# A two-layer attention, Hyena and RWKV-7 step on one core: TensorE's instructions pinned to the source's order

## The chip, the cores and the metric

The kernel runs on one core of a Trainium2 chip. The core has five engines that each work through an instruction stream of their own: TensorE (matmuls and transposes), VectorE and ScalarE (elementwise work), GpSimd (here mainly memsets and DMA issues) and SyncE (here DMA issues). They meet through semaphores. In the profile they are PE, DVE, ACT, POOL and SP. The metric is the device time of one execution in microseconds.

## The reference

One inference step of a backbone with two layers, on 128 context tokens and 128 latent tokens of width 2048, in fp32. The part that matters:

```python
def _layer(x, cond, p, ctx):
    sh1, sc1, g1, sh2, sc2, g2 = _modulation(cond, p['ada_w'], p['ada_b'])   # silu(cond) @ ada_w + ada_b, 6 vectors
    h = _rmsnorm(x, nw[0]) * (1.0 + sc1) + sh1
    o, st = _mixer(h, p, ctx)
    x = x + g1 * _rmsnorm(o, nw[1])
    h = _rmsnorm(x, nw[2]) * (1.0 + sc2) + sh2
    f = jnp.square(jax.nn.relu(h @ p['mlp_w1'])) @ p['mlp_w2']
    return x + g2 * _rmsnorm(f, nw[3]), st

def _mixer(h, p, ctx):
    u = h @ p['w_in']                       # one input projection
    att = ...   # 12 heads, 4 kv heads, softmax with a sink
    hy = _hyena(u_hy, p)                    # long convolution; its filter is sin(sin(feat @ f1) @ f2) @ f3
    rw, S_fin = _rwkv(...)                  # 12 heads, a scan over 128 tokens in each direction
    return jnp.concatenate([att, hy, rw], -1) @ p['w_out'], ...
```

## The kernel before

Both token groups are handled together, as two sets of 128 rows. A weight product is done in three passes, since each fp32 operand is split into a rounded high part and a rest: `acth` and `actl` (or `osh`, `osl`, `fh`, `fl`) for activations, `wh` and `wl` for weights. `wload` brings a block of weights by DMA from SyncE into `wr`; ScalarE rounds it to `wh` (line 219) and VectorE subtracts to get `wl` (line 220). `ws` (lines 481 to 501) multiplies with 256 columns per matmul, `as_` (lines 503 to 519) with 512. Both are generators that yield after each contraction tile. Their results are the PSUM tiles `mm`, of which there are two; all small steps use `sm` tiles, of which there are three.

The stages follow each other: boot (modulation vectors of layer 0 and the first norm), mixer 0, norm, MLP 0, norm, mixer 1, norm, MLP 1. A norm (line 455) works in eight groups: VectorE scales a piece `xn`, TensorE transposes it in four instructions (line 466), and ScalarE and VectorE make `acth` and `actl` from it. The products of the next stage need all eight groups only for their last contraction tiles.

In a mixer the weight products are the main stream, and everything small runs beside it. `Side` holds generators for the small chains: the Hyena filter (line 550: a matmul, a sine, a matmul, a sine, two matmuls at lines 567, 571 and 579), attention, the Hyena convolution, and RWKV. `run` (line 1089) walks through a weight product and after each contraction tile calls `Side.step`, which lets the generators write their next piece, and `ada_step`, which writes the modulation matmuls (`ada`, lines 374 to 376, eight at a time with 32 output rows each). The rates stand in `OPTS` (line 108). A generator that yields a number is left alone for so much work of the main stream.

RWKV goes in two batches of three blocks of 128 channels per layer. `rwkv_stage1` (line 804) does a block: low-rank products (lines 820 and 828), a chain of tanh, running sums and exponentials on VectorE and ScalarE, two small matmuls (lines 845 and 850), two scaled copies `rkf` (line 874), their transposes (line 880), and products of 64-row tiles (line 904, four in a group). `rwkv_stage2` (line 980) then reads the inverted blocks back as `rXT` by DMA and runs groups of 32 by 32 tiles (lines 1001 and 1003); `rwkv_out` (line 1033) normalises and transposes the result (line 1061).

This source order is not the order of execution. A scheduler takes the program as written with its data dependences and its own estimate of durations, and may put instructions of an engine in another order where no dependence stands against it. Before, that holds for every engine, TensorE too. Each engine then works through its stream in the order given to it.

Of the kernel before, what the change touches and what calls it, by code (L numbers as in the profile page):

```python
# [18 lines left out]
KT = 16  # L19
# [137 lines left out]

class Kern:
    def __init__(self, tc, es, A, O, opts=None):
# [6 lines left out]
        self.side = Side()  # L166
        self.adaq = deque()
# [56 lines left out]
    def setup(self):  # L224
# [17 lines left out]
        nc.tensor.transpose(ps[:, 0:32], th[:], self.ident[0:32, 0:32])  # L242
# [21 lines left out]
    def params(self, l):  # L264
# [34 lines left out]
        for i, gr in enumerate(groups):  # L299
# [3 lines left out]
            nc.tensor.transpose(ps[:, 0:n], rows[:], self.ident[0:n, 0:n])  # L303
# [17 lines left out]
    def ada_group(self, l, P, i, cg):  # L321
# [4 lines left out]
        for kq in range(8):  # L326
# [5 lines left out]
            else:  # L332
                w.append(t)
                for j in range(4):
                    m = nc.tensor.matmul(ps[32 * j:32 * j + 32, :], lhsT=self.cs[:, 2 * (kq - 1) + j, :], rhs=w[j // 2][:, j % 2, :],
                                         start=(kq == 1), stop=(kq == 7))
# [6 lines left out]
        for j in range(4):  # L343
            nc.tensor.matmul(pv[:, j, :], lhsT=rows[:, j * 128:(j + 1) * 128], rhs=self.cst("selq"), start=True, stop=True)
# [16 lines left out]
    def ada_vector(self, l, P, i):  # L361
# [4 lines left out]
        for k in range(KT):  # L366
            for h in range(2):
# [3 lines left out]
                if len(w) == 4:  # L371
                    for kk in (k - 1, k):
                        for j in range(4):
                            nc.tensor.matmul(ps[32 * j:32 * j + 32, :], lhsT=self.cs[:, kk, :],  # L374
# [17 lines left out]
        else:  # L392
# [4 lines left out]
            for q in range(4):  # L397
                nc.tensor.matmul(pv[:, q], lhsT=rows[:, q * 128:(q + 1) * 128], rhs=self.cst("sel8").rearrange("p (j c) -> p j c", c=2),
# [56 lines left out]
    def norm(self, P, parts, isc, ish, act):  # L455
# [3 lines left out]
        for c in range(4):  # L459
            for g in range(2):  # L460
# [4 lines left out]
                for j in range(4):  # L465
                    nc.tensor.transpose(pv[:, j, :], xn[:, j * 128:(j + 1) * 128], self.ident)
# [14 lines left out]
    def ws(self, act, w, widths, ps):  # L481
# [4 lines left out]
        for kq in range(KT // nk):  # L486
            hi, lo = self.wload(w[kq * nk * 128:(kq + 1) * nk * 128, :], nk, ncol)
            for kk in range(nk):
# [3 lines left out]
                for b, wd in enumerate(widths):  # L492
                    o = ps[0:wd, b * 256:(b + 1) * 256]
                    h, lw = hi[:, kk, c0:c0 + wd], lo[:, kk, c0:c0 + wd]
                    m = nc.tensor.matmul(o, lhsT=h, rhs=hh, start=(k == 0 and b % 2 == 0), stop=False, skip_group_check=True)  # L495
                    if b == 0 and kk == 0:
                        self.anchors.append(m.ins.name)
                    nc.tensor.matmul(o, lhsT=h, rhs=hl, start=False, stop=False, skip_group_check=True)  # L498
                    nc.tensor.matmul(o, lhsT=lw, rhs=hh, start=False, stop=(k == KT - 1), skip_group_check=True)  # L499
# [3 lines left out]
    def as_(self, lhs, ks, w, ncol, ps):  # L503
# [3 lines left out]
        for i0 in range(0, len(ks), nk):  # L507
            hi, lo = self.wload(w[ks[i0] * 128:(ks[i0] + nk) * 128, :], nk, ncol)
            for kk in range(nk):
                first, last = i0 + kk == 0, i0 + kk == len(ks) - 1  # L510
                for g in range(2):
                    hh, hl = (a[:, g * 128:(g + 1) * 128] for a in lhs[ks[i0 + kk]])
                    o = ps[:, g * 512:g * 512 + ncol]
                    m = nc.tensor.matmul(o, lhsT=hh, rhs=hi[:, kk, :], start=first, stop=False)  # L514
                    if g == 0 and kk == 0:
                        self.anchors.append(m.ins.name)
                    nc.tensor.matmul(o, lhsT=hh, rhs=lo[:, kk, :], start=False, stop=False)  # L517
                    nc.tensor.matmul(o, lhsT=hl, rhs=hi[:, kk, :], start=False, stop=last)  # L518
# [31 lines left out]
    def hyena_filter(self, l):  # L550
# [16 lines left out]
        nc.tensor.matmul(ps[0:64, 0:128], lhsT=f1[:], rhs=self.cst("featt")[0:33, :], start=True, stop=True)  # L567
# [3 lines left out]
        nc.tensor.matmul(ps[0:64, 0:128], lhsT=f2[:], rhs=h1[:], start=True, stop=True)  # L571
# [799 lines left out]
```

## Time and profile before

| what | value |
|---|---|
| median of 3 runs | 2949.42 us (2944.27 to 2960.29) |
| the profiled execution, its own time | 2948.62 us |
| its span in the trace | 2946.8 us |
| TensorE busy | 2833.7 us, 96% of the span |
| VectorE busy | 1651.4 us, 56% |
| ScalarE busy | 1230.8 us, 42% |
| GpSimd busy | 177.5 us, 6% |
| mean DMA rate | 222 GB/s |

The profiled execution lies within the spread of the runs; 1.8 us of its time lie outside the span. The page gives busy time per engine, the chain of work that ended last, and groups of instructions; the trace behind it can be asked for single instructions with start and duration, with the idle time before them and who ended it, and for the busy time in any stretch. The granted clock is a share of TensorE's full clock of 2.4 GHz: 1.00 is 2.4 GHz and 0.50 is 1.2 GHz. A matmul's duration overlaps the next one's start, so the price of one in a row is the distance between starts.

### The profile page before, as it was taken

How to read it: one execution, taken by the hardware profiler on the slowest of the kernel's cores; microseconds unless marked ns; L12 is line 12 of the kernel's file. 1: busy time of each engine (PE TensorE's matmuls, PEld its weight loads, DVE VectorE, ACT ScalarE, POOL GpSimd, SP SyncE). 2: the span in 40 equal slices, each digit the busy share in tenths (PEclk: the TensorE clock that was granted, in tenths of full speed). 3: DMA queues.
4: the chain of work that ended last, by engine and by line, in shares of the span. 5: the costliest groups of instructions: out<-in, count | busy, mean ns of one | idle time of the engine just before them, and what ended most of it. 6: DMA issues, size and time to landing. Idle time of an engine off the chain costs nothing.

```text
span 2946.8 us, 47852 instructions
## 1 busy us (share of the span) xinstructions
PE 2833.7 (96%) x19163; PEld 2318.8 (79%) x19163; DVE 1651.4 (56%) x2627; ACT 1230.8 (42%) x1870; POOL 177.5 (6%) x368
## 2 busy tenths in 40 slices
PE   6899999999899999999999999999879999999998
PEld 2586787767797797897876978887669989889896
DVE  1356666776654344444446576776775545545555
ACT  2354345434543343343335454453355444444343
POOL 0011101201000000000000111011000000000000
PEclk9999899999999999999999998998889999999999
DMA  9985575477888888888898744533455666666674
GB/s 337 333 296 185 188 253 157 137 258 275 296 280 288 275 287 274 299 283 281 284 334 274 232 135 114 147 93 95 138 189 170 188 187 186 186 187 186 188 240 150
DMA packets 326057, 654.56 MB, mean 222 GB/s; under 512 B 48581, under 2 KB 86030, under 8 KB 325707
## 3 DMA queue, kind: packets, MB, share of 16 engines
q1 hardware_dynamic: 311328, 610.88, 64.0%
q0 software_dynamic: 12928, 36.98, 3.8%
q10 hardware_dynamic: 1579, 3.64, 0.3%
q8 instruction: 150, 2.46, 0.3%
q14 instruction: 72, 0.59, 0.1%
HBM read 632.21 MB, written 19.20 MB: 221 GB/s over the span
## 4 chain that ended last, share of the span: by engine, by line
PE 86%; DVE 5%; DMA 5%; ACT 2%; issue 1%; SPq 0%; POOL 0%; DVEq 0%; ACTq 0%; POOLq 0%
PE mm L495 12%; PE mm L499 12%; PE mm L498 12%; PE mm L514 11%; PE mm L517 11%; PE mm L518 11%; PE ada L374 5%; PE sm L904 2%; DMA wa<-in_ada_w_dram 2%; PE sm L925 1%; PE sm L1003 1%; DVE wl L220 1%; PE sm L1018 1%; PE sm L1001 1%; DMA wr<-in_ada_w_dram 1%
## 5 line engine op out<-in xcount | busy, mean ns | idle before, releaser
L220 DVE TENSOR_TENSOR wl<-wr,wh 128x1024 fp32r<-128x1024 f32 (+1 forms) x784 | 928.1, 1185 | 931.2 <-ACT wh L219 910.0
L219 ACT CAST wh<-wr 128x1024 fp32r<-128x1024 f32 (+1 forms) x784 | 796.5, 1017 | 1169.3 <-PE mm L498 545.6
L495 PE MATMUL mm<-acth,wh 128*128 128x256 f32 (+1 forms) x3200 | 914.4, 286 | 11.5 <-ACT acth L476 9.2
L499 PE MATMUL mm<-acth,wl 128*128 128x256 f32 (+1 forms) x3200 | 907.1, 283 | 2.4 <-DVE wl L220 2.4
L498 PE MATMUL mm<-actl,wh 128*128 128x256 f32 (+1 forms) x3200 | 907.5, 284 | 0.3 <-DVE actl L477 0.3
L495 PEld LDWEIGHTS mm<-acth,wh 128*128 128x128 f32 (+1 forms) x3200 | 605.2, 189 | 56.3 <-issue 23.8
L499 PEld LDWEIGHTS mm<-acth,wl 128*128 128x128 f32 (+1 forms) x3200 | 605.2, 189 | 8.3 <-DVE wl L220 3.4
L498 PEld LDWEIGHTS mm<-actl,wh 128*128 128x128 f32 (+1 forms) x3200 | 605.4, 189 | 3.9 <-issue 2.5
L517 PE MATMUL mm<-wl,fh 128*128 128x512 f32 x1024 | 408.0, 398 | 0.3 <-DVE wl L220 0.3
L514 PE MATMUL mm<-wh,fh 128*128 128x512 f32 x1024 | 406.6, 397 | 0.0
L518 PE MATMUL mm<-wh,fl 128*128 128x512 f32 x1024 | 402.4, 393 | 0.0
L514 PEld LDWEIGHTS mm<-wh,fh 128*128 128x128 f32 x1024 | 191.8, 187 | 67.6 <-ACT wh L219 10.9
L518 PEld LDWEIGHTS mm<-wh,fl 128*128 128x128 f32 x1024 | 192.3, 188 | 45.7
L517 PEld LDWEIGHTS mm<-wl,fh 128*128 128x128 f32 x1024 | 192.4, 188 | 43.8 <-DVE wl L220 0.8
L374 PE MATMUL ada<-wa,cs 128*32 128x512 f32 x1280 | 180.6, 605 | 9.2 <-DMA wa<-in_ada_w_dram 9.1
L514 PE MATMUL mm<-wh,osh 128*128 128x512 f32 x256 | 108.8, 425 | 3.4 <-ACT osh L1172 3.4
L517 PE MATMUL mm<-wl,osh 128*128 128x512 f32 x256 | 105.0, 410 | 3.4 <-DVE wl L220 3.4
L518 PE MATMUL mm<-wh,osl 128*128 128x512 f32 x256 | 103.0, 402 | 0.0
L374 PEld LDWEIGHTS ada<-wa,cs 128*32 128x32 f32 x1280 | 35.3, 109 | 84.9 <-issue 54.2
L904 PE MATMUL sm<-rZR,rKB 64*128 64x256 f32 x384 | 83.8, 456 | 0.7 <-DVE rLA L908 0.3
L514 PE MATMUL mm<-wh,acth 128*128 128x512 f32 (+1 forms) x192 | 74.8, 389 | 0.0
L517 PE MATMUL mm<-wl,acth 128*128 128x512 f32 (+1 forms) x192 | 69.1, 360 | 0.0
(323 smaller groups left out, 2598.2 us busy)
## 6 DMA issues: line engine op xcount, KB each, us to landing
wr<-in_mlp_w_dram SPq DMA_DIRECT2D x512, 512.0 KB
wa<-in_ada_w_dram SPq DMA_DIRECT2D x352, 512.0 KB
wr<-in_w_in_dram SPq DMA_DIRECT2D x96, 512.0 KB
wr<-in_w_in_dram SPq DMA_DIRECT2D x112, 384.0 KB
wr<-in_w_out_dram SPq DMA_DIRECT2D x64, 512.0 KB
wr<-in_ada_w_dram SPq DMA_DIRECT2D x32, 512.0 KB
gb<-gate POOLq DMA_DIRECT2D x16, 512.0 KB, 8.9
xd<-acc SPq DMA_DIRECT2D x24, 256.0 KB
```

Of the source, the lines that this page charges most:

```text
L219: nc.scalar.copy(hi, raw)
L220: nc.vector.tensor_sub(lo, raw, hi)
L374: nc.tensor.matmul(ps[32 * j:32 * j + 32, :], lhsT=self.cs[:, kk, :], rhs=w[2 * (kk - k + 1) + j // 2][:, 512 * (j % 2):512 * (j % 2) + 51 ...
L495: m = nc.tensor.matmul(o, lhsT=h, rhs=hh, start=(k == 0 and b % 2 == 0), stop=False, skip_group_check=True)
L498: nc.tensor.matmul(o, lhsT=h, rhs=hl, start=False, stop=False, skip_group_check=True)
L499: nc.tensor.matmul(o, lhsT=lw, rhs=hh, start=False, stop=(k == KT - 1), skip_group_check=True)
L514: m = nc.tensor.matmul(o, lhsT=hh, rhs=hi[:, kk, :], start=first, stop=False)
L517: nc.tensor.matmul(o, lhsT=hh, rhs=lo[:, kk, :], start=False, stop=False)
L518: nc.tensor.matmul(o, lhsT=hl, rhs=hi[:, kk, :], start=False, stop=last)
L904: nc.tensor.matmul(ps[h][:, i * 256:(i + 1) * 256], lhsT=KB[hs, d, g, i, :], rhs=ZR[hs, d, g, :, :].rearrange("p i t -> p (i t)"), start=T ...
L925: nc.tensor.matmul(o[:, 64 * h:64 * h + 64], lhsT=R.MA[d][h][:, 0:128] if i == 0 else MY[h][:], rhs=vT[:, g, 64 * h:64 * h + 64], start=fi ...
L1001: nc.tensor.matmul(o, lhsT=LA[d][:, gh, qs[d]], rhs=G[:, d, gh, :], start=True, stop=True)
```

## The change

A small class `Ordered` wraps `nc.tensor.matmul` and `nc.tensor.transpose`. Each instruction issued through it gets an edge to the one issued before it. The edge is of order alone (`NoSync`): it emits no semaphore and no wait, it only tells the scheduler that the second may not be put ahead of the first. Every matmul and transpose of the kernel is now called as `self.te.matmul` or `self.te.transpose`; nothing else is edited. TensorE's stream is so the order in which the source writes it, and the other engines' streams are still the scheduler's.

```diff
+class Ordered:
+    def __init__(self, tc):
+        self.tc, self.last = tc, None
+
+    def queue(self, i):
+        if self.last is not None:
+            self.tc.add_manual_dep(i.ins, self.last, mybir.DependencyInfo(mybir.DependencyClass.NoSync, mybir.DependencyReason.DATA),
+                                   reason="order")
+        self.last = i.ins.name
+        return i
+
+    def matmul(self, *a, **k):
+        return self.queue(self.tc.nc.tensor.matmul(*a, **k))
+
+    def transpose(self, *a, **k):
+        return self.queue(self.tc.nc.tensor.transpose(*a, **k))
...
         self.side = Side()
+        self.te = Ordered(tc)
...
                 for j in range(4):
-                    nc.tensor.transpose(pv[:, j, :], xn[:, j * 128:(j + 1) * 128], self.ident)
+                    self.te.transpose(pv[:, j, :], xn[:, j * 128:(j + 1) * 128], self.ident)
```

The number of matmuls is the same. 13386 of 16811 keep their very position in TensorE's stream; the others move by at most 228 places. The moves lie in the boot, in the two mixers and in the norms. In the changed kernel every matmul is issued from line 172 and every transpose from line 175.

The first place is the norm ahead of the second MLP, on TensorE. `xn` is the scaled piece, `acth`, `actl`, `wh` and `wl` belong to the MLP's first product. Before:

```order
L466 MATMUL sm_20976<-const_66,xn_20974 128x128 x4
L466 MATMUL sm_20990<-const_66,xn_20988 128x128 x4
L466 MATMUL sm_21004<-const_66,xn_21002 128x128 x4
L495 MATMUL mm_21092<-acth_20954,wh_21094 128x256
L466 MATMUL sm_21018<-const_66,xn_21016 128x128 x4
L498 MATMUL mm_21092<-actl_20955,wh_21094 128x256
L499 MATMUL mm_21092<-acth_20954,wl_21095 128x256
L495 MATMUL mm_21092<-acth_20954,wh_21094 128x256
L498 MATMUL mm_21092<-actl_20955,wh_21094 128x256
L499 MATMUL mm_21092<-acth_20954,wl_21095 128x256
L495 MATMUL mm_21092<-acth_20954,wh_21094 128x256
L498 MATMUL mm_21092<-actl_20955,wh_21094 128x256
```

After, at the same place:

```order
L175 MATMUL sm_20976<-const_66,xn_20974 128x128 x4
L175 MATMUL sm_20990<-const_66,xn_20988 128x128 x4
L175 MATMUL sm_21004<-const_66,xn_21002 128x128 x4
L175 MATMUL sm_21018<-const_66,xn_21016 128x128 x4
L175 MATMUL sm_21032<-const_66,xn_21030 128x128 x4
L175 MATMUL sm_21046<-const_66,xn_21044 128x128 x4
L175 MATMUL sm_21060<-const_66,xn_21058 128x128 x4
L175 MATMUL sm_21074<-const_66,xn_21072 128x128 x4
L172 MATMUL mm_21092<-acth_20954,wh_21094 128x256
L172 MATMUL mm_21092<-actl_20955,wh_21094 128x256
```

The products that stood between the last five groups of transposes (55 up to the eighth group) now stand behind all eight.

The second place is the Hyena filter of layer 0, on TensorE. `hf` are its small weights, `hh` is what the sine chain gives. Before, its second matmul stands 60 rows behind the first, among the mixer's first products:

```order
L495 MATMUL mm_1066<-acth_107,wh_1196 128x256
L498 MATMUL mm_1066<-actl_108,wh_1196 128x256
L499 MATMUL mm_1066<-acth_107,wl_1197 128x256
L571 MATMUL sm_1116<-hh_206_1108,hf_199_1081 64x128
L495 MATMUL mm_1066<-acth_109,wh_1233 128x256
L498 MATMUL mm_1066<-actl_110,wh_1233 128x256
```

After:

```order
L172 MATMUL sm_1098<-const_66,hf_198_1079 64x128
L172 MATMUL mm_1066<-acth_103,wh_1068 128x256
L172 MATMUL mm_1066<-actl_104,wh_1068 128x256
L172 MATMUL mm_1066<-acth_103,wl_1069 128x256
L172 MATMUL mm_1066<-acth_103,wh_1068 128x256
L172 MATMUL mm_1066<-actl_104,wh_1068 128x256
L172 MATMUL mm_1066<-acth_103,wl_1069 128x256
L172 MATMUL sm_1116<-hh_206_1108,hf_199_1081 64x128
```

Six products stand between the filter's first and second matmul now, and six more between the second and the third.

The third place is the end of the first RWKV block of layer 0, on TensorE. `rkf` are the scaled copies, `rZR` and `rKB` the operands of the 64-row products. Before:

```order
L514 MATMUL mm_1737<-wh_1974,acth_109 128x512
L880 MATMUL sm_1958<-const_66,rkf_1944 128x128 x2
L904 MATMUL sm_1991<-rZR_1938,rKB_1939 128x256
L880 MATMUL sm_1958<-const_66,rkf_1956 128x128 x2
L904 MATMUL sm_1992<-rZR_1938,rKB_1939 128x256
L904 MATMUL sm_1991<-rZR_1938,rKB_1939 128x256
L904 MATMUL sm_1992<-rZR_1938,rKB_1939 128x256
L517 MATMUL mm_1737<-wl_1975,acth_109 128x512
```

After:

```order
L175 MATMUL sm_1958<-const_66,rkf_1944 128x128 x2
L175 MATMUL sm_1958<-const_66,rkf_1956 128x128 x2
L172 MATMUL mm_1737<-wh_1974,acth_109 128x512
L172 MATMUL mm_1737<-wl_1975,acth_109 128x512
L172 MATMUL mm_1737<-wh_1974,actl_110 128x512
L172 MATMUL mm_1737<-wh_1974,acth_109 128x512
L172 MATMUL mm_1737<-wl_1975,acth_109 128x512
L172 MATMUL mm_1737<-wh_1974,actl_110 128x512
L172 MATMUL sm_1991<-rZR_1938,rKB_1939 128x256
L172 MATMUL sm_1992<-rZR_1938,rKB_1939 128x256
L172 MATMUL sm_1991<-rZR_1938,rKB_1939 128x256
L172 MATMUL sm_1992<-rZR_1938,rKB_1939 128x256
```

The four 64-row products stand together and behind both transposes, and the transposes stand 31 rows behind the low-rank products, where they stood 38 and 40 behind. In all, the stream changes the tile shape between neighbours 628 times before and 557 times after; 19 of 48 groups of line 904 have other matmuls between their four before, none after.

## Rows read from the trace of the kernel before

**Rows 1.** The page: the chain that ended last, share by engine.

```profile
PE 86%; DVE 5%; DMA 5%; ACT 2%; issue 1%; SPq 0%; POOL 0%; DVEq 0%; ACTq 0%; POOLq 0%
```

**Rows 2.** Busy time by stage (columns in the first line): mixer 0, MLP 0, mixer 1.

```profile
core 0: us, PE busy (x) PEld busy (x) DVE busy (x) ACT busy (x) POOL busy (x), PEclk, DMA share, GB/s
...
148.00:736.00 588.00, 572.86 (x4162) 435.83 (x4161) 391.83 (x798) 247.59 (x469) 76.89 (x160) 0.97 0.65 218
...
772.00:1576.00 804.00, 804.00 (x5261) 660.23 (x5260) 369.50 (x387) 306.12 (x340) 12.52 (x23) 1.00 0.85 287
...
1606.00:2189.00 583.00, 560.90 (x4071) 466.84 (x4070) 402.53 (x806) 263.54 (x485) 70.13 (x146) 0.94 0.47 144
```

**Rows 3.** Timeline, TensorE (start, us, instruction); busy time in the last norm.

```profile
148.55 0.28 PE L499 MATMUL mm<-acth,wl 128*128 128x256 f32 x1
148.67 0.28 PE L495 MATMUL mm<-acth,wh 128*128 128x256 f32 x1
...
2206.60:2217.20 10.60, 10.54 (x71) 0.79 0.02 3
```

**Rows 4.** Timeline of the Hyena filter, TensorE and ScalarE: layer 0, then layer 1.

```profile
147.85 0.43 PE L567 MATMUL sm<-const,hf 33*64 33x128 f32 x2
155.19 0.31 ACT L547 ACTIVATE hh<-snx 64x128 f32<-64x128 f32 x1
155.55 0.43 PE L571 MATMUL sm<-hh,hf 64*64 64x128 f32 x2
158.62 0.31 ACT L547 ACTIVATE hh<-snx 64x128 f32<-64x128 f32 x1 [2.03 <-DVE snx L545]
...
1609.83 0.43 PE L571 MATMUL sm<-hh,hf 64*64 64x128 f32 x2
1616.75 0.31 ACT L547 ACTIVATE hh<-snx 64x128 f32<-64x128 f32 x1
```

**Rows 5.** First and last of twelve RWKV blocks; waits (total, times, longest us).

```profile
220.47 1.03 PE L828 MATMUL sm<-rad,rup 96*128 96x256 f32 x4
231.86 0.51 ACT L874 ACTIVATE rkf<-rKB,rI 128x256 f32<-128x256 f32 x1
...
2019.40 1.03 PE L828 MATMUL sm<-rad,rup 96*128 96x256 f32 x4
2029.72 0.51 ACT L874 ACTIVATE rkf<-rKB,rI 128x256 f32<-128x256 f32 x1 [0.23 <-DVE rKB L872]
...
PE sm L880 <- ACT rkf L874: 8.8, 10, 2.1
```

**Rows 6.** Timeline, TensorE: 64-row groups, 512-column products, modulation matmuls (x2 is one).

```profile
232.33 0.70 PE L904 MATMUL sm<-rZR,rKB 64*128 64x256 f32 x2
...
233.32 1.13 PE L904 MATMUL sm<-rZR,rKB 64*128 64x256 f32 x6
...
234.96 0.40 PE L514 MATMUL mm<-wh,acth 128*128 128x512 f32 x1
235.19 0.40 PE L517 MATMUL mm<-wl,acth 128*128 128x512 f32 x1
...
235.74 1.13 PE L904 MATMUL sm<-rZR,rKB 64*128 64x256 f32 x8
...
524.62 1.92 PE L374 MATMUL ada<-wa,cs 128*32 128x512 f32 x16
637.43 1.06 PE L374 MATMUL ada<-wa,cs 128*32 128x512 f32 x8
...
1616.81 1.04 PE L374 MATMUL ada<-wa,cs 128*32 128x512 f32 x2
```

**Rows 7.** Timeline, TensorE (in brackets: idle time before, and who ended it).

```profile
1862.57 0.52 PE L725 MATMUL sm<-const,ape 128*128 128x128 f32 x2 [0.82 <-DVE ape L718]
...
2111.15 0.82 PE L1003 MATMUL sm<-rG,rXT 32*32 32x64 f32 x6 [1.21 <-DMA rXT<-rdout]
...
2166.56 0.44 PE L1061 MATMUL sm<-const,rYc 128*128 128x128 f32 x2 [1.62 <-DVE rYc L1054]
```

**Rows 8.** Busy time in a late stretch of mixer 1 (columns as in rows 2).

```profile
1996.00:2016.00 20.00, 19.79 (x57) 12.64 (x58) 9.51 (x23) 2.46 (x8) 0.75 (x1) 0.50 0.28 93
```

More of the change, by code (lines that the diff above doesn't have):

```diff
@@ L343, in ada_group @@
         for j in range(4):
-            nc.tensor.matmul(pv[:, j, :], lhsT=rows[:, j * 128:(j + 1) * 128], rhs=self.cst("selq"), start=True, stop=True)
+            self.te.matmul(pv[:, j, :], lhsT=rows[:, j * 128:(j + 1) * 128], rhs=self.cst("selq"), start=True, stop=True)
         self.ada_mod(P, i, P.mod[i][:, 4 * cg:4 * cg + 4, :], pv, slice(4 * cg, 4 * cg + 4))
@@ L566, in hyena_filter @@
         ps = self.sm()
-        nc.tensor.matmul(ps[0:64, 0:128], lhsT=f1[:], rhs=self.cst("featt")[0:33, :], start=True, stop=True)
+        self.te.matmul(ps[0:64, 0:128], lhsT=f1[:], rhs=self.cst("featt")[0:33, :], start=True, stop=True)
         h1 = self.sin_(ps[0:64, 0:128], bb[:, 0:1], "hh1")
@@ L570, in hyena_filter @@
         ps = self.sm()
-        nc.tensor.matmul(ps[0:64, 0:128], lhsT=f2[:], rhs=h1[:], start=True, stop=True)
+        self.te.matmul(ps[0:64, 0:128], lhsT=f2[:], rhs=h1[:], start=True, stop=True)
         h2 = self.sin_(ps[0:64, 0:128], bb[:, 1:2], "hh2")
@@ L591, in hyena_filter @@
             ps = self.sm()
-            nc.tensor.matmul(ps[:], lhsT=self.cst(m), rhs=src[:], start=True, stop=True)
+            self.te.matmul(ps[:], lhsT=self.cst(m), rhs=src[:], start=True, stop=True)
             H = sb([128, 512], F32, tag="hHs")
@@ L819, in rwkv_stage1 @@
         for d in range(2):
-            nc.tensor.matmul(ps[:, d * 256:(d + 1) * 256], lhsT=wu[:, d, :], rhs=P.tw[:, d * 256:(d + 1) * 256], start=True, stop=True)
+            self.te.matmul(ps[:, d * 256:(d + 1) * 256], lhsT=wu[:, d, :], rhs=P.tw[:, d * 256:(d + 1) * 256], start=True, stop=True)
         th = sb([128, 4, 129], F32, tag="rth")
@@ L844, in rwkv_stage1 @@
         ps = self.sm()
-        nc.tensor.matmul(ps[:, 0:256], lhsT=self.cst("sel6")[0:6, 128 * bi:128 * bi + 128], rhs=P.inv[:], start=True, stop=True)
+        self.te.matmul(ps[:, 0:256], lhsT=self.cst("sel6")[0:6, 128 * bi:128 * bi + 128], rhs=P.inv[:], start=True, stop=True)
         kk = sb([128, 256], F32, tag="rkk")
@@ L849, in rwkv_stage1 @@
         ps = self.sm()
-        nc.tensor.matmul(ps[:, 0:256], lhsT=self.cst("bones"), rhs=rk[:], start=True, stop=True)
+        self.te.matmul(ps[:, 0:256], lhsT=self.cst("bones"), rhs=rk[:], start=True, stop=True)
         bv = sb([128, 256], F32, tag="rbv")
```

76 lines of the change are left out of this document (38 added, 38 removed).

## The prediction

> **What bounds the kernel now.** I read the chain of waits first: 86% of it is TensorE, 5% VectorE, 5% DMA [rows 1]. The busy time by stage then says where TensorE is not solid [rows 2]. The first MLP has no gap (804.00 busy of 804.00 us); the two mixers have gaps of 15.1 us (588.00 less 572.86) and 22.1 us (583.00 less 560.90). So whatever TensorE adds or waits for in a mixer or a norm goes straight to the end. It adds nothing only where a transfer or a VectorE chain ends last anyway, as in the boot.
>
> The program's order on TensorE, compared between the two kernels, is the same in both MLPs (13386 of 16811 matmuls keep their very position) and differs in four places: boot, norms, Hyena filter and the rest of the two mixers. The free scheduler put independent weight products between a step and the step that needs its result. Pinned, each step has only the products that the source writes there. The pin takes no work away. So I count, for each place, the products that stand as cover before and after, and set them against the latency that they cover. For prices I take the spacing of starts: 0.12 us for a product of 256 columns (148.55 to 148.67) [rows 3] and 0.23 to 0.24 us for one of 512 (234.96 to 235.19; I use 0.235) [rows 6].
>
> **Term 1, the norms: +19 us.** Three norms feed products of a next stage (MLP 0, mixer 1, MLP 1). Today 55, 48 and 55 of the next products stand between the eight groups of transposes, which wait one after another for xn from VectorE. After, all eight groups stand first. In the last norm TensorE is busy 10.54 of 10.60 us with 71 instructions while the groups trickle in [rows 3]. Pinned, it idles through that stretch and then still has the products to do: 55 x 0.12 = 6.6 us, and 48 x 0.12 = 5.8 us, 19.0 in all. VectorE's weight splits that stand between its norm steps move behind them and can shorten a norm by 1 or 2 us, so the low bound is 12. The high bound is 25, 2 us of lower clock in each.
>
> **Term 2, the Hyena filter: +13 us.** Each layer runs a small matmul, a sine chain on VectorE and ScalarE, the next small matmul. In layer 0 the first chain lasts from 148.28 (147.85 + 0.43) to 155.50 (155.19 + 0.31), 7.2 us [rows 4]. Before, 60 products stand in it (60 x 0.12 = 7.2, which is why nothing waits); after, 6 (0.7 us): 6.5 us of wait. The second chain lasts from 155.98 to 158.93, 2.95 us less 0.7, 2.3 us. Layer 1 has the longer second one: 1610.26 to 1617.06, 6.8 us, less 24 x 0.12 = 2.9, that is 3.9 us. Sum 12.7, bounds 8 (VectorE reaches the chain sooner, since TensorE's stop holds up the conversions that it now serves in between) and 16.
>
> **Term 3, twelve RWKV blocks: +41 us, the largest.** In a block the low-rank products (line 828) start a VectorE and ScalarE chain that ends with two scaled copies, rkf (line 874), which TensorE transposes (line 880). In the first block the products end at 221.50 and the second rkf at 232.37, 10.9 us; in the last at 2020.43 and 2030.23, 9.8 us [rows 5]. After, a block of a layer's first batch (three blocks) has 24 products of 512 columns (24 x 0.235 = 5.6 us), in the first block also eight modulation matmuls (1.9 us) and two small ones (1.0): 8.5 us, so 2.4 us of wait. A block of the second batch has 36 of 256 columns (4.3 us) and the small ones, 5.3 us: 4.5 us of wait in the last. Done so for all twelve, the waits are 2.4, 2.4, 3.2, 4.2, 7.4, 5.0 in layer 0 and 3.2, 2.1, 3.3, 3.1, 8.8, 4.5 in layer 1: 49.6 us. The waits of this kind that are there today, 8.8 us [rows 5], come off: 41. The low bound is 20: VectorE's order hardly changes, but while TensorE stands still, the foreign Hyena and split work ahead of a chain is thinned out (about half of the 14 us latencies is such work). The high bound is the whole 50.
>
> **Term 4, smaller places: +19 us.** In layer 1's second RWKV stage the 24 small matmuls of line 1003 wait for rXT, a DMA. They start at 2111.15 after a wait of 1.21 us [rows 7]; after, they stand 31 products of 512 columns earlier, 31 x 0.235 = 7.3 us that no longer cover the DMA. The transposes of line 1061 had 12 and 20 such products ahead (2.8 and 4.7 us) and one still waited 1.62 us [rows 7]: I take 3 us each. The softmax transposes at 1862.57 waited 0.82 us [rows 7] and come 73 instructions earlier, some 8 us: I take 6 and bound it by 0 and 9, because the softmax of that head may itself be started earlier. Together 19, from 8 to 24. The boot is moved too, but DMA sets its pace; I take nothing, at most 8.
>
> **Term 5, groups kept whole: -29 us.** The free order drops single matmuls of one kind into groups of another. Of the 64-row groups of line 904 one matmul alone takes 0.70 us and the other three 1.13, where four together take 1.13 [rows 6]: 0.70 lost, in 19 of 48 groups, 13 us. Of the modulation matmuls (32 columns wide, eight in a row) a run of one takes 1.04 us, of four 1.06, of eight 1.92 [rows 6]. 110 of them stand in 35 runs of one to four and 4 runs of seven: 35 x 1.0 + 4 x 1.9 = 42.6, where whole eights would take 110 / 8 x 1.92 = 26.4. That gives back 16. Bounds 20 and 38, the upper one with the transposes that are split too.
>
> The Trainium skill (TensorEngine Tiling (Array Packing), Key Properties) says that a change of tiling mode drains TensorE; the trace agrees in that one lone 64-row matmul takes 0.70 us. By that rule alone the change is a gain, since the pinned order has 557 such changes where the free one has 628.
>
> **Term 6, the clock: +15 us.** In 1996.00 to 2016.00 TensorE was busy 19.79 of 20.00 us at a granted clock of 0.50, its level of 1.2 GHz [rows 8], and waits of TensorE stand ahead of it. Such a stretch costs half its length, here 10 us. The new waits are short and spread over places that are partly slow already. I take one and a half such stretches; the bounds are 0 and 40, four more.
>
> The Trainium skill (TensorE: Matmul & The Clock Gate, Part 1) calls the throttled clock the default that activity releases; that speaks against a change that adds idle time, and the trace agrees with 0.50 in that stretch.
>
> **Sum.** 19 + 13 + 41 + 19 - 29 + 15 = +78 us on the profiled execution, whose span is 2946.8 and whose own time is 2948.6; the median is 2949.4, so the two bases agree. 2948.6 + 78 = 3026.6, I say 3027. All low bounds together (12 + 8 + 20 + 8 - 38 + 0 = +10) give 2959, all high ones (25 + 16 + 50 + 24 + 8 - 20 + 40 = +143) 3092.
>
> **The rivals.**
> Clock worse than taken: each of the twelve block waits and the three norms lets the clock fall once more. Five more stretches at 10 us come to about +55 over the forecast's term, around 3080. For it: layer 1's gaps are 7 us longer than layer 0's and its granted clock is 0.94 to 0.97 [rows 2]. Against: the waits are 2 to 9 us, much like those that are there today.
>
> Waits absorbed: VectorE catches up while TensorE stands, so the chain after the next wait is shorter, and the terms 1 to 4 shrink to about 35 us against 29 given back: about 2955, no change that can be told (a measurement of this kernel tells about 0.5%, 15 us). For it: in the long latencies half is foreign work. Against: foreign work has to be done somewhere, and its order on VectorE is as before.
>
> Whole groups win, faster: one mechanism, broken groups of lines 904 and 374, price up to 38 us [rows 6]. It decides if the added waits and clock come to less than 23 us; with 15 us of them the time is 2926. For it: TensorE is the chain, so a gain there is paid out in full. Against: norms and filters alone give 32, from counts that leave little room.
>
> The pin does nothing: TensorE would have to be in the source's order already. The listing shows 3400 matmuls elsewhere, so I give it no chance of its own.
>
> **How the numbers follow.** Forecast (2985 to 3065) 0.58; clock worse (above 3065) 0.14; milder waits, half of terms 1 to 4 (2964 to 2985) 0.10; no change (2934 to 2964) 0.08; faster by over 0.5% 0.10. Slower by over 0.5% is then 0.82. The time is the forecast's, 3027. For the range I leave out the faster case and a part of no change (about 0.13 below 2955) and the end of the clock case (about 0.07 above 3090).
>
> **What would show it.** Term 1: each norm in the new trace shows eight groups of transposes with idle time before them and no product in between; TensorE busy well below half there. Term 2: waits of several us for hh, which does not stand among today's waits. Term 3: the waits for rkf come to 40 to 50 us in place of 8.8; if they stay below 20, the absorption rival is right. Term 4: a wait of about 8 us for rXT. Term 5: the line 904 groups all as x8 of about 1.13 us, and modulation runs of eight at 1.9. Term 6: the granted clock of the mixers at or below 0.95 and 0.93. Wrong if TensorE's order turns out to be free after all, if the idle time in the MLPs (where nothing moved) grows, or if the boot, which I set at nothing, becomes longer.

## The result

The pinned kernel takes 3028.62 us in the median of 4 runs (3025.99 to 3031.45), the kernel before 2948.24 us beside it (2944.27 to 2960.29). The ratio is 1.0263, with an interval of 1.0240 to 1.0286: slower by 78 us (71 to 84). The prediction was 3027 us, with a range of 2955 to 3090.

The page of the pinned kernel: busy time by engine, and the granted clock in 40 slices.

```profile
PE 2821.8 (93%) x19163; PEld 2324.3 (77%) x19163; DVE 1653.4 (55%) x2627; ACT 1235.9 (41%) x1871; POOL 178.6 (6%) x368
...
PEclk8889999999899999999998999998898999999999
```

TensorE's busy time fell by 12 us, from 2833.7 to 2821.8, and its span grew by 83, from 2946.8 to 3029.7. So the loss is idle time (113 us before, 208 now), and TensorE's own work became a little cheaper. The waits of the pinned kernel say where (TensorE's instruction, whom it waited for, total us, times, longest):

```profile
PE sm L175 <- ACT rkf L895: 42.6, 23, 7.3
PE sm L175 <- DVE xn L483: 32.0, 19, 11.4
PE sm L175 <- DVE rYc L1075: 20.3, 4, 6.4
PE sm L172 <- DMA rXT<-rdout: 10.5, 5, 3.6
...
PE sm L172 <- ACT hh L568: 10.1, 3, 5.0
...
PE sm L172 <- DVE o L663: 4.8, 1, 4.8
```

The first row answers to the last of [rows 5]: 8.8 us before, 42.6 now. hh and o were not waited for at all before. For the transposes of xn, for rYc and for rXT the kernel before has these rows:

```profile
PE sm L466 <- DVE rs L448: 11.4, 1, 11.4
...
PE sm L466 <- DVE xn L462: 2.8, 3, 1.5
...
PE sm L1061 <- DVE rYc L1054: 1.8, 2, 1.6
PE sm L1003 <- DMA rXT<-rdout: 1.6, 2, 1.2
```

The longest wait for xn (11.4 us) is therefore no cost of the pin: it stands at the head of the last norm, and the kernel before has it too, put down there to rs. The waits for xn rose from 14.2 us to 32.0, by 18.

The busy time by stage (columns as in [rows 2]; mixer 0, MLP 0, mixer 1, each between its own bounds):

```profile
154.10:770.80 616.70, 564.95 (x4170) 437.12 (x4174) 391.35 (x797) 251.51 (x470) 77.57 (x160) 0.95 0.62 209
801.10:1619.20 818.10, 818.10 (x5367) 673.41 (x5369) 375.46 (x397) 312.00 (x350) 12.58 (x23) 1.00 0.84 284
1645.40:2264.10 618.70, 563.14 (x4147) 470.70 (x4145) 407.06 (x814) 266.84 (x490) 68.45 (x142) 0.94 0.46 137
```

The gaps in the two mixers are 52 us (616.70 less 564.95) and 56 us, against 15 and 22 in [rows 2]. Measured between the same instructions (first filter matmul of layer 0, or end of the norm, to the last output product), mixer 0 took 588 us before and 617 after, mixer 1 586 and 619. The MLPs, where nothing moved, still have no gap.

The last norm looks like this in the timeline, TensorE (start, duration, instruction, idle time before it):

```profile
2275.42 1.97 PE L175 MATMUL sm<-const,xn 128*128 128x128 f32 x8 [11.36 <-DVE xn L483]
2278.86 1.12 PE L175 MATMUL sm<-const,xn 128*128 128x128 f32 x4 [1.47 <-DVE xn L483]
2281.46 1.09 PE L175 MATMUL sm<-const,xn 128*128 128x128 f32 x4 [1.48 <-ACT xnt L493]
2282.78 1.09 PE L175 MATMUL sm<-const,xn 128*128 128x128 f32 x4 [0.23 <-DVE xn L483]
...
2290.55 0.42 PE L172 MATMUL mm<-actl,wh 128*128 128x256 f32 x1
2290.76 0.41 PE L172 MATMUL mm<-acth,wl 128*128 128x256 f32 x1
```

Eight groups of transposes stand with idle time between them and no product (the first row holds two groups). The wait of 11.36 us ahead of them is not new; the first line below shows it in the kernel before. The two other lines are the busy time from the first transpose to the end of the last (columns as in [rows 2]), before and now:

```profile
2201.07 1.94 PE L466 MATMUL sm<-const,xn 128*128 128x128 f32 x8 [11.45 <-DVE rs L448]
```

```profile
2201.07:2217.87 16.80, 14.24 (x89) 13.22 (x90) 12.49 (x27) 10.72 (x22) 0.00 (x0) 0.70 0.10 29
```

```profile
2275.42:2290.55 15.13, 8.53 (x34) 6.28 (x34) 11.78 (x28) 9.31 (x20) 0.00 (x0) 0.50 0.07 28
```

The stretch itself became 1.7 us shorter. What it costs is the products that now follow it, and the clock: they begin 0.21 us apart, where two such products stand 0.12 apart in [rows 3], since the clock is at its lower level (0.50) through the whole norm. Before, it rose within the norm (0.70 in the mean).

What became cheaper are the groups (busy time of their rows: line, instruction, busy us, mean ns, idle before), pinned kernel first, then the kernel before:

```profile
L172 PE MATMUL ada<-wa,cs 128*32 128x512 f32 x1280 | 162.2, 611 | 8.0 <-DMA wa<-in_ada_w_dram 8.0
L172 PE MATMUL sm<-rZR,rKB 64*128 64x256 f32 x384 | 62.3, 427 | 3.7 <-DVE rLA L929 3.6
```

```profile
L374 PE MATMUL ada<-wa,cs 128*32 128x512 f32 x1280 | 180.6, 605 | 9.2 <-DMA wa<-in_ada_w_dram 9.1
L904 PE MATMUL sm<-rZR,rKB 64*128 64x256 f32 x384 | 83.8, 456 | 0.7 <-DVE rLA L908 0.3
```

The 64-row products fell by 21.5 us and the modulation matmuls by 18.4. That is 40 us, and all of TensorE's work fell by 12 only. So about 28 us went the other way, in rows whose work is the same; the mean granted clock is 0.958, against 0.973 before.

### The profile page after: what moved, and what is told of

The parts are those of the page before. It is cut to its first block, busy times and chain, and to the rows that moved or that the text cites. A ratio compares the mean times of both kernels' runs of the same rounds, so it can differ in the third digit from the quotient of the medians.

```text
span 3029.7 us, 47863 instructions
## 1 busy us (share of the span) xinstructions
PE 2821.8 (93%) x19163; PEld 2324.3 (77%) x19163; DVE 1653.4 (55%) x2627; ACT 1235.9 (41%) x1871; POOL 178.6 (6%) x368
## 3 DMA queue, kind: packets, MB, share of 16 engines
q1 hardware_dynamic: 311328, 610.88, 62.3%
## 5 line engine op out<-in xcount | busy, mean ns | idle before, releaser
L172 PE MATMUL mm<-acth,wh 128*128 128x256 f32 (+1 forms) x3200 | 927.6, 290 | 10.8 <-ACT wh L240 6.0
L172 PEld LDWEIGHTS mm<-wh,fh 128*128 128x128 f32 x1024 | 191.5, 187 | 67.6 <-ACT wh L240 10.9
L172 PE MATMUL ada<-wa,cs 128*32 128x512 f32 x1280 | 162.2, 611 | 8.0 <-DMA wa<-in_ada_w_dram 8.0
L928 DVE COPY_PREDICATED rMA<-masks,sm 128x256 f32<-128x256 uint8 x96 | 42.3, 441 | 51.8 <-PE sm L172 51.1
L172 PE MATMUL mm<-wh,actl 128*128 128x512 f32 (+1 forms) x192 | 70.3, 366 | 0.0
```

The costliest lines, as they stand in the source:

```text
L172: return self.queue(self.tc.nc.tensor.matmul(*a, **k))
L928: nc.vector.copy_predicated(R.MA[d][h], mk[d], ps[h][:, 0:256])
```

## The experiments

**Freeing parts of the pinned kernel.** Three kernels take the pin off one part and leave the rest pinned; a fourth gives the free kernel whole groups of modulation matmuls.

The boot left free:

```diff
...
-        if self.last is not None:
+        if self.on and self.last is not None:
...
+        self.te.on = True
         for l in range(DEPTH):
```

> The pinned kernel with TensorE left free in the boot alone (edges from the first mixer on). Reading of the two traces: the end of the boot lies 20 us later in the pinned kernel, because a matmul that waits for one weight block holds those behind it, and the blocks' buffers come free later. Theory: 3029 - 20 = about 3009 (3000 to 3015). Rival, the boot's delay is caught up by the transfers anyway, so that freeing it only moves the wait into the mixer: 3022 to 3032.

Measured: 3021.20 us, ratio to before 1.0238 (1.0199 to 1.0277). Against 1.0263 that is no gain that can be told. My reading of the traces was at fault: the 20 us stood at an instruction inside the boot, and by its end most of them were caught up. The first matmul of the filter, behind the boot, tells it (kernel before in its second trace, pinned kernel, boot left free; [rows 4] has 147.85 for the first trace of before):

```profile
152.14 0.43 PE L567 MATMUL sm<-const,hf 33*64 33x128 f32 x2
```

```profile
154.11 0.43 PE L172 MATMUL sm<-const,hf 33*64 33x128 f32 x2
```

```profile
155.44 0.43 PE L172 MATMUL sm<-const,hf 33*64 33x128 f32 x2
```

The norms' transposes left free:

```diff
-                    self.te.transpose(pv[:, j, :], xn[:, j * 128:(j + 1) * 128], self.ident)
+                    (self.te if boot else nc.tensor).transpose(pv[:, j, :], xn[:, j * 128:(j + 1) * 128], self.ident)
...
```

> The pinned kernel with the transposes of the three later norms left free, so that products may stand between them again. Theory: the waits for xn, 32.0 us pinned and 14.2 us free, go back, and a little lower clock with them: 3029 - 18 to 24 = 3005 to 3011. Rival, VectorE's own chain sets the length of a norm and the products only fill it without shortening the time: 3022 to 3032.

Measured: 3015.59 us, ratio 1.0211 (1.0167 to 1.0256), some 15 us less than the pinned kernel by the two ratios. In the trace norm 1 with mixer 1 takes 11 us less than pinned, norm 2 with the second MLP 7, norm 0 with the first MLP 3, while the boot and mixer 0 take 5 more. The direction is the theory's, but the time lies between the theory's range and the rival's: the waits for xn went back to 22.3 us, not to 14.2.

Every TensorE instruction of the RWKV functions left free:

```diff
-                self.te.transpose(ps[:, (2 * d + i) * 128:(2 * d + i + 1) * 128], kf[d][:, i, :], self.ident)
+                nc.tensor.transpose(ps[:, (2 * d + i) * 128:(2 * d + i + 1) * 128], kf[d][:, i, :], self.ident)
...
```

> The pinned kernel with every TensorE instruction of the RWKV functions left free, the rest pinned. Theory: the waits for rkf (42.6 us pinned, 8.8 free), rYc (20.3 and 1.8) and rXT (10.5 and 1.6) go, 61 us, and the 64-row groups are broken again, which gives back up to 20 us: 2975 to 3000. Rival, VectorE's chains absorb most of the waits, so that they turn up as other waits: 3010 to 3030.

Measured: 2986.79 us, ratio 1.0116 (1.0077 to 1.0155), in the theory's range. The wait for rkf and the 64-row products in its trace:

```profile
PE sm L901 <- ACT rkf L895: 8.5, 10, 2.7
...
L925 PE MATMUL sm<-rZR,rKB 64*128 64x256 f32 x384 | 84.7, 456 | 0.3 <-DVE rLA L929 0.3
```

The wait for rkf is back at 8.5 us (and that for rXT at 0.9), and the groups are broken again: 84.7 us against 62.3. One part of the theory failed: the wait for rYc fell only from 20.3 to 15.9 us.

```profile
PE sm L1082 <- DVE rYc L1075: 15.9, 3, 6.4
```

Waits and groups change together here, so what the whole groups are worth in time in the pinned kernel this run does not tell.

The kernel before, with the modulation groups begun by the block that is loaded last, so that the free order keeps more of them whole (8 of 80 are broken in the program, 15 before):

```diff
-                    for kk in (k - 1, k):
-                        for j in range(4):
+                    for kk in (k, k - 1):
+                        for j in (3, 2, 1, 0):
...
-                                             start=(kk == 0), stop=(kk == KT - 1))
+                                             start=(kk == 1), stop=(kk == KT - 2))
```

> The kernel before, TensorE free, with one thing of the pinned order: the modulation matmuls stand in whole groups, because each group begins with the matmul of the block that is loaded last. Theory (broken groups cost about 1 us per fragment, 16 us in all): 2949 - 12 to 16 = 2933 to 2937. Rival, a fragment costs nothing because TensorE would have waited there: 2944 to 2952.

Measured: 2951.94 us in 10 runs, ratio 1.0010 (0.9989 to 1.0030). The row of the modulation matmuls fell as foreseen, and nothing came of it:

```profile
L374 PE MATMUL ada<-wa,cs 128*32 128x512 f32 x1280 | 162.5, 621 | 10.1 <-DMA wa<-in_ada_w_dram 10.1
```

180.6 to 162.5 us is the same saving as in the pinned kernel, and the time stayed, as the rival has it. Its reason holds in part: TensorE's busy time fell by only 9 us in all (2833.7 to 2824.5 on the page), and its idle time rose by 12. The other part is the clock. The ten executions have a mean granted clock of 0.964 to 0.969, the 13 of the kernel before beside them 0.965 to 0.973 (median 0.971). To see what that costs, weigh each us of an execution by its clock, that is, multiply its span by its mean clock; I call this its time at full clock. For the kernel before it is 2862 us (mean), here 2853, 9 us less. What is left of the span, 87 us before and 98 here, is 11 us more.

**Paying for the waits in two ways.** Does the wait itself cost, or what comes with it? One kernel writes cover into the source, the other fills the waits with useless matmuls.

```diff
         h1 = self.sin_(ps[0:64, 0:128], bb[:, 0:1], "hh1")
-        yield
+        yield 2.5
...
         h2 = self.sin_(ps[0:64, 0:128], bb[:, 1:2], "hh2")
-        yield
+        yield 2
...
             kf.append(sb([128, 2, 128], F32, tag="rkf"))
...
-            yield
+            yield 1.5 * d
...
+    def among(self, norm, g):
+        for n, _ in enumerate(norm):
+            for _ in range(4 if n else 0):
+                next(g)
...
-                for _ in self.norm(p, parts, 1, 0, act):
-                    pass
+                self.among(self.norm(p, parts, 1, 0, act), first[0][1])
...
-            for _ in self.norm(p, parts, 4, 3, act):
-                pass
+            self.among(self.norm(p, parts, 4, 3, act), m0[1])
...
```

> The pinned kernel with cover written into the source at three places: twelve contraction tiles of the next product among the norm's transposes, a delay of 2.5 and 2 units of main products behind the two sines of the Hyena filter, one of 1.5 units ahead of the transposes of rkf. Theory (the pinned order costs what its places leave uncovered: xn 35.0 less 14.3, hh 10.0, rkf 42.6 less 8.9 us idle, and some lower clock with them): 3029 - 55 to 75 = 2954 to 2974. Rival, the chains on VectorE and ScalarE are what sets the length of the mixers, and a later step only moves the wait to the end of the mixer: 3000 to 3030.

Measured: 3018.56 us, ratio 1.0222 (1.0189 to 1.0255), some 12 us less than the pinned kernel by the two ratios and in the rival's range. The theory is right in kind for the norms and wrong for the mixers. The waits of its trace and its stages (mixer 0, MLP 0, mixer 1):

```profile
PE sm L172 <- DMA rXT<-rdout: 18.3, 3, 14.8
PE sm L175 <- ACT rkf L895: 11.3, 6, 6.0
...
PE sm L175 <- DVE ape L739: 9.4, 5, 4.4
```

```profile
158.20:782.80 624.60, 584.34 (x4251) 443.57 (x4251) 389.61 (x797) 245.76 (x467) 81.54 (x168) 0.95 0.66 223
817.30:1620.50 803.20, 803.20 (x5255) 660.10 (x5257) 370.29 (x394) 307.44 (x347) 13.28 (x26) 1.00 0.84 286
1652.70:2257.90 605.20, 552.69 (x4018) 463.69 (x4016) 404.01 (x812) 259.98 (x486) 71.79 (x148) 0.93 0.43 132
```

In the norms the cover works. From the end of mixer 1 to the end of the program, where no other work moved, the kernel takes 758.4 us (3016.3 less 2257.9) in place of 765.6 (3029.7 less 2264.1), 7 us less. The edit puts eight of its twelve contraction tiles ahead of the eighth group of transposes and four behind it.

In the mixers the wait for rkf is gone to a quarter (42.6 to 11.3 us over both). Mixer 0 takes 624.6 us all the same, 8 more than pinned, but not for new waits: its idle time fell from 52 to 40 us. More of the modulation matmuls run in it, 15 us of them (their busy time alone in mixer 0, pinned, then here):

```profile
154.10:770.80 616.70, 55.18 (x436) 0.95 0.62 209
```

```profile
158.20:782.80 624.60, 70.51 (x516) 0.95 0.66 223
```

In mixer 1 the idle time hardly fell (56 to 53 us): there a wait of 14.8 us for rXT takes the place of the waits removed. I read it so that a step moved back moves the end of its chain too, and that cover in a mixer must come from products moved ahead of the waiting step, as the free order did it. This one wait suggests it; no run tests it.

Useless matmuls in the waits:

```diff
+    def busy(self, ps, n):
+        for _ in range(n):
+            self.te.matmul(ps[:], lhsT=self.ident, rhs=self.const[:, 0:512], start=True, stop=True)
...
+                self.busy(ps, 2 * (not boot))
                 for j in range(4):
                     self.te.transpose(pv[:, j, :], xn[:, j * 128:(j + 1) * 128], self.ident)
...
+        self.busy(ps, 4)
         for d in range(2):
             for i in range(2):
                 self.te.transpose(ps[:, (2 * d + i) * 128:(2 * d + i + 1) * 128], kf[d][:, i, :], self.ident)
...
```

> The pinned kernel with matmuls of constants, whose results are overwritten, ahead of the waiting steps: four of 512 columns (about 2 us) ahead of each block's transposes of rkf, two (about 1 us) ahead of each of the 24 groups of transposes in the later norms. They lie in TensorE's waits and add no wait of their own where the wait is longer. Theory on the clock (part of the loss is the lower granted clock behind waits: transposes of xn 29.1 us against 19.4, products of 256 columns some 15 us more than in the kernel before): the granted clock rises from 0.96 and the time falls by 10 to 25 us, to 3004 to 3019. Rival, the clock costs nothing beyond the waits: 3026 to 3040, since four blocks wait less than 2.5 us.

Measured: 3022.98 us, ratio 1.0243 (1.0202 to 1.0284): not told apart from the pinned kernel in time, with this much more work in it:

```profile
PE 2875.2 (95%) x19355; PEld 2343.5 (77%) x19355; DVE 1652.8 (55%) x2627; ACT 1236.7 (41%) x1871; POOL 178.5 (6%) x368
...
L172 PE MATMUL sm<-const 128*128 128x512 f32 x192 | 89.7, 600 | 0.0
L175 PE MATMUL sm<-const,xn 128*128 128x128 f32 x128 | 20.0, 284 | 10.9 <-DVE xn L487 10.9
L175 PE MATMUL sm<-const,rkf 128*128 128x128 f32 x48 | 8.8, 289 | 9.2 <-ACT rkf L900 9.2
```

The useless matmuls are busy for 89.7 us, and the waits that they fill shrink by 58 us (xn from 35.0 to 10.9, rkf from 42.6 to 9.2). They outlast the waits by some 30 us, and yet the time did not rise. All other TensorE work takes 2875.2 - 89.7 = 2785.5 us, 36 less than the 2821.8 of the pinned kernel, and the mean granted clock rose from 0.958 to 0.970. So the lower clock behind the waits costs the pinned kernel about 30 us of busy time (the rows overlap by some us, so I do not say 36). The time lies between the theory's range and the rival's. Counted at full clock the kernel has 2934 us against 2905 pinned, so the surplus of useless matmuls cost 29 us; what is left of the span fell from 122 to 88 us, so the clock gave back 34. The two nearly cancel.

**The kernel before once more.**

> The kernel before once more, for a second trace of the boot. In its first trace the boot ends 20 us earlier than in the pinned kernel, but the pinned kernel with a free boot did not get this back. If the boot's transfers are faster in some executions than in others: the shares of DMA in 50 to 95 us below 0.95 here, against 0.99, and the start of the mixer 5 to 20 us later, at about the same total. If the first trace is typical: 0.99 again.

One run: 2943.39 us. The DMA share in 50 to 95 us was 0.99 again, and the boot ended 4 us later (the row above). In nine traces with the free boot its end stands at 147.9 to 155.4 us (mean 152.0), in five with the pinned boot at 154.1 to 158.5 (mean 156.4). By these means the boot costs about 4 us. But the two ranges overlap, and the one kernel that differs from the pinned one by the boot alone ended it at 155.4, later than the pinned kernel's 154.1, so this cost is not shown.

**One term at a time, by a table.** These kernels do not pin the source's order but one given by a table: all matmuls are gathered in the source's order, and the edges follow the table's.

```diff
...
     def queue(self, i):
-        if self.last is not None:
-            self.tc.add_manual_dep(i.ins, self.last, mybir.DependencyInfo(mybir.DependencyClass.NoSync, mybir.DependencyReason.DATA),
-                                   reason="order")
-        self.last = i.ins.name
+        self.all.append(i.ins)
         return i
+
+    def close(self):
+        k, row = -1, []
+        for d in zlib.decompress(base64.b85decode(TABLE)).decode().split(","):
+            k += int(d)
+            row.append(self.all[k])
+        for a, b in zip(row, row[1:]):
+            self.tc.add_manual_dep(b, a.name, mybir.DependencyInfo(mybir.DependencyClass.NoSync, mybir.DependencyReason.DATA),
+                                   reason="order")
...
```

With the order of before in the table, the program is that of before, instruction by instruction on all engines: the edges themselves cost nothing. So each of the next kernels is the kernel before with one thing moved on TensorE; the scheduler still orders the other engines around it.

The norms alone (the products behind the eighth group):

> TensorE pinned by a table to the order of before, with the 57, 49 and 55 products that stand among the transposes of the three later norms moved behind the eighth group. Theory (term 1): 2948 + 17 to 26 = 2965 to 2974. Rival, VectorE's weight splits that now come later in the norms shorten them, and the products cost nothing: 2944 to 2956.

Measured: 2967.57 us, ratio 1.0071 (1.0047 to 1.0094): +21 us (14 to 28). The time is the theory's. In its trace 9 us of it are idle time and 12 are busy time for the same work, at a mean clock of 0.967 (span 2967.4 and busy 2845.2 us, against 2946.8 and 2833.7). Its last norm reads as in the pinned kernel:

```profile
2214.03 1.12 PE L187 MATMUL sm<-const,xn 128*128 128x128 f32 x4 [1.48 <-DVE xn L495]
2216.62 1.09 PE L187 MATMUL sm<-const,xn 128*128 128x128 f32 x4 [1.48 <-ACT xnt L505]
```

The transposes of rkf alone:

> TensorE pinned by a table to the order of before, with the transposes of rkf alone moved to where the source has them among the main products, in 11 of 12 RWKV blocks (the twelfth cannot stand there alone). They stand 7, 1, 6, 50, 53, 15, 9, 1, 6, 62 and 37 instructions earlier, some 33 us of products. Theory (term 3 of the prediction: what is no longer covered is waited for): 2948 + 25 to 40 = 2973 to 2988, with rkf waits near 40 us. Rival, the mixers' length is set by VectorE's chain, as the run with cover in the source suggests, and an early wait shortens a later one: 2944 to 2960.

Measured: 2990.90 us, ratio 1.0138 (1.0108 to 1.0167): +41 us (32 to 49). The time is 3 us above the theory's range, and the rival falls:

```profile
PE sm L187 <- ACT rkf L907: 48.5, 21, 9.2
```

48.5 us of wait against 8.8, that is 40 more, and 41 more in the time: no sign that any of it was paid back by a shorter wait. But that the two agree is not the wait's doing alone. With the transposes moved away, nine of the 19 broken groups of line 904 are whole, and their row is cheaper by 12 us (83.8 before); and the mean granted clock is lower, 0.967 to 0.969, where the kernel before has a median of 0.973 beside it:

```profile
L184 PE MATMUL sm<-rZR,rKB 64*128 64x256 f32 x384 | 71.9, 421 | 0.8 <-DVE rLA L941 0.7
```

Most of terms 2 and 4:

> TensorE pinned by a table to the order of before, with these steps alone moved to the source's places: the matmuls of the Hyena filter behind its sines in both layers, the small matmuls of lines 1001 and 1003 of each layer's last RWKV stage 2, and the transposes of rYc (line 1061, with line 1065) of each layer's first RWKV batch. The other steps of terms 2 and 4 cannot stand at the source's places one by one. Theory (what is no longer covered is waited for): idle time for hh 10, rXT 7 to 9, rYc 12 us, so 2946 + 22 to 32 = 2968 to 2978. Rival, these waits are paid back by shorter ones later in the same mixer: 2944 to 2958.

Measured: 2986.82 us, ratio 1.0143 (1.0115 to 1.0171): +42 us (34 to 50), more than the theory's 22 to 32. The waits:

```profile
PE sm L184 <- DMA rXT<-rdout: 16.6, 5, 11.1
PE sm L187 <- DVE rYc L1087: 14.5, 3, 6.4
...
PE sm L184 <- ACT hh L580: 9.9, 4, 5.5
```

hh (9.9) and rYc (14.5) come near what was expected. For rXT 16.6 us stand with one wait of 11.1, where the pinned kernel has 10.5 us and none over 3.6. My reading, not tested: the step was moved to its place in an order whose earlier steps still ran as before, so it met the transfer earlier than in the pinned kernel, and this run overstates that term by 6 us. In all, TensorE's idle time rose by 28 us, as the theory has it (113.1 to 141.5), and its busy time by 9, with the lower clock.

Whole groups alone, at lines 904 and 374:

> TensorE pinned by a table to the order of the kernel before, with one alteration: the groups of line 904 (four) and of the modulation matmuls (eight) are gathered at the place of their last member. (The unaltered table gives the very program of before.) Theory, the gain of whole groups is real and lies on the path: 20 us at line 904 and 16 at the modulation matmuls by the busy time of the pinned kernel, so 2948 - 25 to 36 = 2912 to 2923. Rival, the early fragments stand where TensorE would have waited, and the gain turns into waits, as the modulation groups alone already suggest (no gain at 17 us less busy time): 2940 to 2952.

Measured: 2938.07 us in 10 runs (2917.51 to 2944.94), ratio 0.9965 (0.9945 to 0.9985): 10 us faster (4 to 16). The groups in the profiled execution, which was the fastest of the ten (2917.51 us):

```profile
PE 2789.0 (96%) x19163; PEld 2302.6 (79%) x19163; DVE 1649.2 (57%) x2627; ACT 1231.7 (42%) x1870; POOL 178.0 (6%) x368
...
L184 PE MATMUL ada<-wa,cs 128*32 128x512 f32 x1280 | 161.0, 608 | 7.2 <-DMA wa<-in_ada_w_dram 7.2
L184 PE MATMUL sm<-rZR,rKB 64*128 64x256 f32 x384 | 62.7, 412 | 5.0 <-DVE rLA L941 5.0
```

The time lies between the two ranges. In this execution the busy time fell by 45 us and the span by 31; the median fell by 10. What most executions give back is the clock: the two fastest have a mean granted clock of 0.977 and 0.974, the other eight 0.966 to 0.971. At full clock all ten lie close together, at 2842 to 2851 us (mean 2847), where the kernel before has 2864 beside them. So whole groups save about 17 us at full clock, and most executions lose some of it to the lower clock. Why the clock fell lower, the one trace, of an execution in which it did not, can't tell.

The groups of lines 925, 933 and 1001 as well:

> As the run with whole groups, and the broken groups of lines 925, 933 and 1001 gathered too (24 more groups). Theory: each costs some tenths of a us while broken, 3 to 8 us together below the run with whole groups: 2905 to 2920. Rival, gathering delays their first members, on which VectorE waits: no gain or a loss of up to 5 us against that run.

Measured: 2932.64 us, ratio 0.9951 (0.9929 to 0.9973), above the theory's range: 14 us faster than before (8 to 21), which is the best kernel of this study. Against the run with whole groups the two intervals overlap; whether these 24 groups add anything is not shown.

## Why the prediction was right

The time was foreseen to 2 us. The mechanism, cover that is lost and waited for, is right; that the number is so near is luck, since errors of several terms cancel. Step by step:

- **What bounds the kernel** holds. The MLPs have no gap in either kernel; TensorE's idle time rose by 95 us (113 to 208), the time by 78.
- **Term 1, norms, +19:** right in time, +21 (14 to 28) alone, and the freed norms gave some 15 back. The working is right only in part. Alone it adds 9 us of idle time and 12 us of busy time for the same work, at a lower clock (0.967 against 0.973); the term had no clock in its sum, only in its high bound. Its sign, TensorE busy well below half in each norm, did not come: it is 8.53 of 15.13 us in the last one, with the clock at 0.50 all through. (Its 55, 48 and 55 products are 57, 49 and 55.)
- **Term 2, filter, +13:** right in mechanism. The wait for hh is 10.1 us in the pinned kernel; it was not priced by itself in time.
- **Term 3, RWKV blocks, +41:** right. Alone +41 (32 to 49) with 11 of 12 blocks moved, though that run has nine groups of term 5 made whole as well; in the pinned kernel the wait rose by 34. Its low bound of 20, with VectorE thinning out its foreign work, did not come about.
- **Term 4, smaller places, +19:** the sum was too low (the waits named here come to about 30 us, above its bound of 24), and so were the parts. rYc was set at 6 us and rose by 18; I counted only the 12 and 20 products ahead of it, although four such places wait now. rXT was set at 7 and rose by 9. The softmax, set at +6, fell from 7.1 to 4.6. A wait for o (line 663, 4.8 us) was not foreseen. The boot, set at nothing, may cost some 4; that is not shown.
- **Term 5, whole groups, -29:** under-sized as busy time of the rows, 21.5 + 18.4 = 40 us in place of 13 + 16. As time it depends on the clock that goes with it. Added to the free order it is worth 10 us (4 to 16), some 17 at full clock, and the modulation groups alone nothing, some 9 at full clock. What it is worth in time within the pinned order was not measured.
- **Term 6, the clock, +15:** under-sized, about 30 us of busy time by the run with filled waits, and about 28 by the rows in which the saving of the groups was lost. Terms 5 and 6 were both set too small, at about three quarters and half of what came, and their errors cancel: -29 + 15 = -14 was foreseen, and TensorE's busy time fell by 12. The stretch of [rows 8] shows one thing that the term did not use: TensorE was busy for 19.79 of 20.00 us there, and the clock stayed at 0.50 all the same.

The single runs add up to 21 + 41 + 42 - 10 = 94 us, where 78 were measured. The listed clocks show in which part the sum fails. At full clock (means) the four kernels stand at +7, +27, +20 and -17 us against the kernel before beside them, together 37, and the pinned kernel at +42 (2905 against 2863, the latter over 44 executions). What is left of the span, the share of the lower clock, is +15, +17, +22 and +6, together 60, where the pinned kernel has 38 more (122 against 84). So waits and groups add up to within 5 us, and the lower clock does not: apart, the moves cost more of it than together. This is a count, not an experiment, and the groups made whole in the rkf run are in it twice.

Of the rivals, "whole groups win" fell because the waits came to far more than 23 us, though its mechanism alone is a gain. "Waits absorbed" fell with the run that moves rkf alone: 40 us of wait, and 41 us more time. "Clock worse than taken" was right that the clock's cost had been taken too low, at 15 us for some 30, but not by the 50 and more that it needed (five stretches of 10 us are 50, not its 55). That TensorE drains at a change of tiling mode (the Trainium skill, TensorEngine Tiling (Array Packing), Key Properties) fits the runs in direction: fewer changes, less busy time, 83.8 to 62.3 us at line 904. That alone did not decide.

## What to carry to other kernels

An order of instructions is a stock of cover. Before pinning one, count for each step that waits on another engine what stands between the step and its producer, and set it against the measured latency; here that count gave the two terms that were run alone, norms and rkf, to within their intervals, although part of each was clock or groups and not the wait itself. So price the lower clock behind new waits too; here it was about 30 us of busy time. Pin the order that runs well rather than the one that reads well: a table of the free order, with tiled groups made whole, beat both kernels, the faster of them by 0.5%. And cover a long chain by moving other work ahead; delaying its steps took the waits for rkf away and gained little here.

## What the runs showed of the hardware

A run of matmuls on 32 output rows costs by steps: about 1 us for one to four and 1.9 us for eight ([rows 6]; the 33 runs of one to four in that trace take 1.02 to 1.07 us), so a lone one wastes three quarters of its time. Matmuls whose results nobody reads, 89.7 us of them put into waits, raised the mean granted clock from 0.958 to 0.970 and took some 30 us off the rest of TensorE's work. They paid for themselves within the error of the time, no more.

Most of what sets executions of one kernel apart here is the granted clock. Over 44 executions of the kernel before, the spans lie between 2936 and 2964 us with a mean clock of 0.975 to 0.965, and their product lies within 2857 to 2871 us. A small saving is therefore told better by span times clock than by the time alone: whole groups are 10 us in the median, and 17 by that product.
